# A two-layer decoder trunk: one more left pair and three more right pairs by seven products, runs of sixteen products in conv and gate, second heads three ticks later

## The chip, the cores and the metric

The kernel runs on one core of a Trainium2 chip. The metric is the device time of one execution in microseconds; lower is better. The core has five engines that run their own instruction streams side by side and wait for one another by semaphores: TensorE (PE in the profile; PEld is its weight load), VectorE (DVE), ScalarE (ACT), GpSimd (POOL) and SyncE (SP), which here only issues transfers. Matmuls write to PSUM, a small memory that this kernel divides into eight tiles of 128 x 512 fp32 values (two double tiles `mm2`, three tiles `bank`, one `av`); everything else on the chip lies in SBUF.

## The reference

Two layers; in each the same five steps on 256 tokens of width 2048:

```python
h = _rmsnorm(x, attn_norm_g[l])
proj = h @ w_in[l]
q, k, v, gate_b, gate_c, conv_in = jnp.split(proj, splits, axis=-1)
...
attn = _diff_attention(q, k, v, lam, rel_bias)
...
conv = gate_b * _short_conv(gate_c * conv_in, conv_w[l])
...
x = x + jnp.concatenate([attn, conv.astype(attn.dtype)], axis=-1) @ w_out[l]
...
hm = _rmsnorm(x, mlp_norm_g[l]) @ w_up[l]
x = x + jnp.square(jax.nn.relu(hm)) @ w_down[l]
```

q, k and v are 1024 wide each (8 heads), and so are gate_b, gate_c and conv_in. w_up is 2048 x 8192, w_down 8192 x 2048. All data is fp32 in HBM.

## The kernel before

**Precision.** TensorE multiplies in fp32r. Every operand is split into a rounded part (hi) and what is left (lo), and a product is three matmuls: hi by hi, hi by lo, lo by hi (`TERMS`). A weight tile is loaded by SP, ACT copies it to hi (L302 for most weights, L818 and L844 in the MLP), and DVE subtracts to get lo (L303, L819, L845). `Weights.take()` hands the next pair of tiles to the matmuls and makes tiles some way ahead.

**Ticks.** Work that is not a weight product (norms, transposes, attention) is written as generators. `work.start(generator, wait)` adds one, and each call of `work.tick()` between groups of matmuls steps those that are due. So a number of ticks says behind how many groups of matmuls a piece of side work is put in TensorE's order. The framework orders the instructions of ACT and DVE by itself; each engine runs its order strictly.

**The mixer** (`mixer`, `linear`, `linear_t`). First q, k and v for heads 0 to 3, then for heads 4 to 7 (`linear`, L386). `attention` is started for each half; its scores are matmuls at L604, its softmax output goes through the av matmuls (L648), `an` (L668) and transposes at L677 into `cat` (L681, L682). Then four times gate_C (`gc`) and conv_in (`ci`), and four times gate_B (`gb`), all by `linear_t` (matmuls at L408): per weight tile of four k, eight hi matmuls of 512 columns and eight lo matmuls of 256 columns, with four ticks. The output projection `o` ends the mixer. The second half's attention starts 9 ticks after it is queued (3 + 6 x half).

**The MLP** (`mlp`). The 8192 hidden units are 32 pairs (`NP`) of 2 x 128. For each pair two up columns (`up_part`, L955, runs of sixteen hi and sixteen lo matmuls) give the squared relu in `square` (L972 to L988), which writes h and splits it into f, hi by ACT at L987 and lo by DVE at L988. The left half of the output (columns 0 to 1023) is accumulated along the way, `LAG` = 2 pairs behind: pair j by seven products (Strassen-Winograd on 2 x 2 blocks, 7 x 3 = 21 matmuls, L998, the weight sums made by DVE and split into `b1`, `b2`, `t13`, `t24`), and the last two pairs, 30 and 31, by `ordinary` (L1079, 8 x 3 = 24 matmuls). Products 1 and 6 share one PSUM tile. Between them `seven_onto(0)` (L1058 to L1070) adds the seven accumulators to x: `e1` by ACT at L1060, the others by DVE (L1052), and x += e at L1068.

**The right half** (columns 1024 to 2047). Every pair's f (or h) was stored to DRAM by POOL's queue and comes back as `fb` or `back`. First pairs 30 and 31, then 2 x `BLK` pairs, then the rest of the hidden units as blocks of two pairs for one half of the right columns at a time (`columns`, L1161, 24 matmuls and 4 ticks each). `SEVEN` lists the pairs that go by seven products; the rest go by `ordinary`. Before, `BLK_AT` = (13, 14): layer 0 has 26 pairs, of which 10 by seven, and the blocks (13,0), (14,0), (13,1), (14,1); layer 1 has 28 pairs, of which 11 by seven, and (14,0), (14,1). In layer 0 the transposes of the next layer's norm (`Norm.chunk`, L454, 8 transposes a chunk into two buffers of the PSUM pool `bank`, which holds three) come among these blocks and the next q projection; `nT` (ACT L270, DVE L271) reads them out of PSUM. Chunks 0 and 1 are of the left half and are started with 4 and 8 ticks ahead of the blocks; chunks 2 and 3 are started when the blocks of their half are done, and wait 5 and 2 ticks. A chunk waits 2 ticks of its own after its start where no other number is written.

**SBUF shared between stages.** `uraw`, the raw tiles of w_up, lie in a pool that is opened for the MLP, in memory that the mixer's temporaries held. SP issues a load when its memory is free, and holds the loads behind it in program order meanwhile.

Of the kernel before, what the change touches and what calls it, by code (L numbers as in the profile page):

```python
# [30 lines left out]
KG = 4  # L31
# [3 lines left out]
LAG = 2  # L35
NB2 = DFF // (KG * P)


SEVEN_AT = (2, 4, 7, 9, 12, 14, 17, 19, 22, 24, 27)
BLK_AT = (13, 14)  # L40

TERMS = ((0, 0), (0, 1), (1, 0))
REL = 2 * S - P - 1
# [62 lines left out]
def trunk(ctx: ExitStack, tc: tile.TileContext, x, w_in, w_out, conv_w, q_norm_g, k_norm_g,  # L106
# [285 lines left out]
    def linear_t(name, acts, weights):  # L392

        acc = mm.tile([P, 2, 2, S], F32, tag="mm2", name=name)
        nk = len(acts) * KG
        for k0 in range(0, nk, 4):
            hi, lo = weights.take()  # L400
            a = acts[k0 // KG]
            while not a.ready:
                work.tick()
            for part, wt in ((0, hi), (1, lo)):
                for k in range(k0, k0 + 4):
                    for f in range(2):
                        fs = slice(f * P, (f + 1) * P)
                        nc.tensor.matmul(  # L408
                            acc[:, f, 0] if part else acc[:, f], wt[:, k % 4, fs],
                            a.ap[:, 0, k % KG] if part else a.ap[:, :, k % KG],  # L410
                            start=(part == 0 and k == 0), stop=(part == 1 and k == nk - 1),
                            skip_group_check=True)
                    if k % 2:
                        work.tick()
        return acc

# [299 lines left out]
    def mixer(l, norm, loads):  # L716

        with ExitStack() as scope:
# [28 lines left out]
            for half in range(2):  # L747
                h0 = 4 * half
                acc = linear(f"q{l}{half}", hT, weights)
                r = norm.r  # L750
                qT = bpool.tile([P, 2, 4, S], F32R, tag="b", name=f"qT{l}{half}")
                work.start(qk_norm(acc, r, q_parts(qT), q_gain[:, l:l + 1], f"q{l}{half}"))
                acc = linear(f"k{l}{half}", hT, weights)
                kT = bpool.tile([P, 2, 4, S], F32R, tag="b", name=f"kT{l}{half}")
                work.start(qk_norm(acc, r, k_parts(kT, kL), k_gain[:, l:l + 1], f"k{l}{half}"))
                acc = linear(f"v{l}{half}", hT, weights)
                v = bpool.tile([P, 2, NT, CH], F32R, tag="b", name=f"v{l}{half}")
                for t in range(NT):
                    nc.scalar.activation(v[:, 0, t], acc[:, t], AF.Copy, scale=r[:, t:t + 1])
                    nc.vector.scalar_tensor_tensor(v[:, 1, t], acc[:, t], r[:, t:t + 1],  # L760
                                                   v[:, 0, t].bitcast(F32),
                                                   op0=ALU.mult, op1=ALU.subtract)
                work.start(attention(l, qT, kT, kL, v, h0, cat[half], bias, tmp,
                                     1 + half), 3 + 6 * half)
            cv = bpool.tile([P, AW // P, S], F32, tag="b", name=f"cv{l}")
            for q in range(AW // WC):
                acc = linear_t(f"gc{l}{q}", hT, weights)
# [22 lines left out]
    def mlp(l, mnorm, last):  # L790

        norm = None if last else Norm(0, l + 1)
        BLK = BLK_AT[l]
        SEVEN = [i for i in SEVEN_AT if i < 2 * BLK]
        mT = mnorm.tiles
        with ExitStack() as scope:
            upool = scope.enter_context(tc.tile_pool(name="upool", bufs=4))
# [86 lines left out]
            for i in range(NP):  # L884
# [6 lines left out]
                for c in range(2):  # L891
                    column(i, c, 0)
                    column(i, c, 1)
                    if i >= LAG:
                        weights.jobs += (pair[2:], pair[:2])[c == 0]
            for i in range(NP - LAG, NP):
                box = []
                rows(i, 0, box)
                rows(i, 1, box)

# [65 lines left out]
            def square(i, h):  # L968


                u = h[:, 0:4].rearrange("p a c -> p (a c)")
                nc.scalar.activation(u, u, AF.Relu)  # L972
                top = h[:, 0:4].rearrange("p (k t) c -> p k t c", t=2)[:, :, 0]
                nc.vector.tensor_mul(top, top,
                                     mnorm.ratio.unsqueeze(1).to_broadcast([P, 2, P]))
                nc.scalar.activation(u, u, AF.Square)
                n = 4
                if i < NP - LAG:
                    n = 8
                    nc.vector.tensor_add(h[:, S1], h[:, A21], h[:, A22])  # L980
                    nc.vector.tensor_sub(h[:, S2], h[:, S1], h[:, A11])
                    nc.vector.tensor_sub(h[:, S3], h[:, A11], h[:, A21])
                    nc.vector.tensor_sub(h[:, S4], h[:, A12], h[:, S2])
                if i in SEVEN:
                    nc.gpsimd.dma_start(hid7[i], h.rearrange("p a c -> p (a c)"))
                f = fpool.tile([P, 2, 8, P], F32R, tag="f", name="f")
                nc.scalar.activation(f[:, 0, :n], h[:, :n], AF.Copy)  # L987
                nc.vector.tensor_sub(f[:, 1, :n], h[:, :n], f[:, 0, :n].bitcast(F32))  # L988
                if i in hid:
                    nc.gpsimd.dma_start(hid[i], f[:, :, 0:4].rearrange("p a k c -> p a (k c)"))  # L990
                return f
# [3 lines left out]
            def product(n, f, a, b, start, stop):  # L995

                for m, (pa, pw) in enumerate(TERMS):
                    nc.tensor.matmul(prods[n], f[:, pa, a], b[pw],  # L998
                                     start=(start and m == 0), stop=(stop and m == 2))

            fs = {}
            for i in range(NP):
                j = i - LAG
                end = i == NP - 1
                h = fpool.tile([P, 8, P], F32, tag="h", name="h", bufs=2)
                if i == 0:
                    two = mm.tile([P, 2, CH], F32, tag="mm2", name="up0")
# [10 lines left out]
                for c in range(2):  # L1018
# [8 lines left out]
                    if j == 0 and c == 0:  # L1027
# [2 lines left out]
                            prods[pair[0]], prods[pair[1]] = w2[:, 0], w2[:, 1]  # L1030
                        for n in (5, 7, 4):
                            prods[n] = bank(f"pr{l}{n}")
                    if j >= 0 and c == 0:
                        b11, b21, b22 = weights.take()
                        t1, t3 = weights.take()
                        f = fs[j]
                        product(1, f, A11, b11, j == 0, end)
                        product(2, f, A12, b21, j == 0, False)
                        product(3, f, S4, b22, j == 0, False)
                        product(5, f, S1, t1, j == 0, end)  # L1040
                        work.tick()
                    elif j >= 0:
                        t2, t4 = weights.take()
                        f = fs[j]
                        product(7, f, S3, t3, j == 0, end)
                        product(6, f, S2, t2, j == 0, end)
                        product(4, f, A22, t4, j == 0, False)
                        work.tick()


            def onto(dst, p, base):
# [20 lines left out]
            def ordinary(f, starts=(), stop=False):  # L1072


                for k in range(2):
# [6 lines left out]
                                stop=(stop and k == 1 and m == 2))  # L1082
                    work.tick()

            add = seven_onto(0)
            prods[8] = ps.tile([P, CH], F32, tag="av", name=f"pr{l}8", bufs=1)
            for j in range(NP - LAG, NP):
                ordinary(fs[j], (8,) if j == NP - LAG else (), j == NP - 1)
            add()
            for n in range(2):  # L1090
                for t in range(NT):
# [176 lines left out]
```

## Time and profile before

| | |
|---|---|
| runs | 2133.83, 2133.86, 2135.43 us, median 2133.86 |
| the profiled execution | 2133.02 us, span of the trace 2131.2 us |
| busy share of the span | PE 100%, PEld 85%, DVE 79%, ACT 63%, POOL 8% |
| DMA | 476.01 MB, mean 223 GB/s, q1 (SP) 60.5%, q0 (POOL) 10.1% |

The span runs from the first to the last instruction in the trace; the execution's time has 1.8 us more around it. In rows of the timeline the columns are start in us from the span's start, duration in us, engine, line, operation, output<-inputs by the program's names, shapes and count; in square brackets stands idle time of that engine ahead of it and what ended it. Matmuls are pipelined: a duration of 0.39 for a 512-column matmul is longer than the distance of two of them. Of the waits, the columns are total in us, times, and the longest.

### The profile page before, as it was taken

The numbers are of one execution on the slowest core, as the hardware profiler recorded it, in microseconds if no ns is written. First come the engines' busy times: TensorE is split into PE (matmuls) and PEld (weight loads), VectorE is DVE, ScalarE is ACT, GpSimd is POOL, SyncE is SP. The second block draws the span as 40 slices with busy tenths as digits, with TensorE's granted clock in tenths as the row PEclk, the third lists the DMA queues.
The fourth block names the chain that finished last, engine by engine and source line by source line (L and its number), as shares of the span: only waits on it lengthen the run. The fifth ranks groups of instructions, "written<-read, shape, count | busy, mean of one in ns | idle before, by whom it ended". The sixth has DMA issues, their size and how long they took to land.

```text
span 2131.2 us, 29207 instructions
## 1 busy us (share of the span) xinstructions
PE 2125.1 (100%) x10925; PEld 1818.4 (85%) x10925; DVE 1693.9 (79%) x2316; ACT 1349.2 (63%) x1776; POOL 165.6 (8%) x226
## 2 busy tenths in 40 slices
PE   9999999999999999999999999999999999999999
PEld 8888888888888888888888888888888888888887
DVE  6778655798888888798766786557988888888986
ACT  6666545677777777656565665446777777675654
POOL 3110100000000000011111101000000000000110
PEclk9999999999999999999999999999999999999999
DMA  8555766677777777788656558656877777777983
GB/s 271 178 166 167 252 193 187 206 252 229 230 236 229 233 235 229 255 297 287 216 170 182 163 162 264 188 178 211 259 231 233 232 235 229 236 229 259 319 297 112
DMA packets 298255, 476.01 MB, mean 223 GB/s; under 512 B 12708, under 2 KB 193782, under 8 KB 298113
## 3 DMA queue, kind: packets, MB, share of 16 engines
q1 hardware_dynamic: 269120, 406.76, 60.5%
q0 software_dynamic: 28800, 67.24, 10.1%
q8 instruction: 85, 1.39, 0.3%
q14 instruction: 58, 0.47, 0.1%
q10 hardware_dynamic: 192, 0.15, 0.0%
HBM read 440.52 MB, written 33.58 MB: 222 GB/s over the span
## 4 chain that ended last, share of the span: by engine, by line
PE 99%; ACT 1%; DVE 0%; issue 0%; DVEq 0%; ACTq 0%
PE upc L955 31%; PE pr L998 14%; PE dn L1079 8%; PE o L386 8%; PE ci L408 4%; PE gb L408 4%; PE k L386 4%; PE q L386 4%; PE v L386 4%; PE gc L408 4%; PE dn L1161 2%; PE dn L998 2%; PE pr1r L998 1%; PE pr0r L998 1%; PE up L955 1%; PE upw L955 1%
## 5 line engine op out<-in xcount | busy, mean ns | idle before, releaser
L303 DVE TENSOR_TENSOR wlo<-raw,whi 128x1024 fp32r<-128x1024 f32 x274 | 343.0, 1252 | 217.8 <-ACT whi L302 213.6
L302 ACT ACTIVATE whi<-raw 128x1024 fp32r<-128x1024 f32 x274 | 290.4, 1060 | 303.3 <-PE o L386 73.6
L955 PE MATMUL upc<-nT,uhi 128*128 128x512 f32 x1920 | 454.7, 389 | 0.0
L955 PEld LDWEIGHTS upc<-nT,uhi 128*128 128x128 f32 x1920 | 360.3, 188 | 74.7
L819 DVE TENSOR_TENSOR ulo<-uraw,uhi 128x1024 fp32r<-128x1024 f32 x256 | 311.9, 1222 | 119.1 <-ACT f L987 91.4
L818 ACT ACTIVATE uhi<-uraw 128x1024 fp32r<-128x1024 f32 x256 | 270.5, 1057 | 159.9 <-PE upc L955 137.5
L955 PEld LDWEIGHTS upc<-nT,ulo 128*128 128x128 f32 x1920 | 246.2, 191 | 9.3
L955 PE MATMUL upc<-nT,ulo 128*128 128x256 f32 x1920 | 249.1, 283 | 0.0
L1079 PE MATMUL dn<-whi,fb 128*128 128x512 f32 x528 | 166.1, 389 | 0.0
L386 PE MATMUL o<-whi,cat 128*128 128x512 f32 x512 | 159.5, 390 | 0.0
L302 ACT ACTIVATE whi<-uraw 128x1024 fp32r<-128x1024 f32 x66 | 70.1, 1062 | 94.0 <-PE dn L1079 77.5
L1079 PEld LDWEIGHTS dn<-whi,fb 128*128 128x128 f32 x528 | 99.1, 188 | 20.6
L844 ACT ACTIVATE b2h<-draw 128x1024 fp32r<-128x1024 f32 x81 | 85.9, 1061 | 45.9 <-PE pr L998 41.3
L386 PEld LDWEIGHTS o<-whi,cat 128*128 128x128 f32 x512 | 96.2, 188 | 19.7
L965 ACT ACTIVATE ev<-upc 128x512 f32<-128x512 f32 x120 | 72.0, 600 | 54.1 <-PE upc L955 54.1
L1079 PE MATMUL dn<-wlo,fb 128*128 128x512 f32 x264 | 102.7, 389 | 0.0
L303 DVE TENSOR_TENSOR wlo<-uraw,whi 128x1024 fp32r<-128x1024 f32 x66 | 80.7, 1223 | 24.8 <-ACT whi L302 24.5
L844 ACT ACTIVATE t24h<-t 128x1024 fp32r<-128x1024 f32 x81 | 86.2, 1064 | 22.2 <-PE pr L998 15.8
L845 DVE TENSOR_TENSOR b2l<-draw,b2h 128x1024 fp32r<-128x1024 f32 x81 | 98.5, 1217 | 1.7 <-ACT b2h L844 1.7
L845 DVE TENSOR_TENSOR t24l<-t,t24h 128x1024 fp32r<-128x1024 f32 x81 | 98.7, 1219 | 1.3
L386 PE MATMUL o<-wlo,cat 128*128 128x512 f32 x256 | 99.6, 389 | 0.0
L845 DVE TENSOR_TENSOR t13l<-t,t13h 128x1024 fp32r<-128x1024 f32 x81 | 98.7, 1219 | 1.1
(408 smaller groups left out, 4153.3 us busy)
## 6 DMA issues: line engine op xcount, KB each, us to landing
uraw<-in_w_up_dram SPq DMA_DIRECT2D x128, 1024.0 KB, 6.2
raw<-in_w_in_dram SPq DMA_DIRECT2D x191, 512.0 KB, 3.8
draw<-in_w_down_dram SPq DMA_DIRECT2D x170, 512.0 KB, 5.2
uraw<-in_w_down_dram SPq DMA_DIRECT2D x66, 512.0 KB, 5.3
raw<-in_w_out_dram SPq DMA_DIRECT2D x64, 512.0 KB, 3.6
hid0p<-f POOLq DMA_DIRECT2D x20, 512.0 KB, 3.6
raw<-in_w_down_dram SPq DMA_DIRECT2D x10, 1024.0 KB, 5.1
fb<-hid0p POOLq DMA_DIRECT2D x20, 512.0 KB, 7.4
```

What stands on the lines that cost most here:

```text
L302: pair = (nc.scalar.activation(hi, raw, AF.Copy), nc.vector.tensor_sub(lo, raw, hi.bitcast(F32)))
L303: nc.vector.tensor_sub(lo, raw, hi.bitcast(F32)))
L386: nc.tensor.matmul(acc[:, t], a.ap[:, pa, k % KG, t * P:(t + 1) * P], (hi, lo)[pw][:, j], start=(k == 0 and n == 0), stop=(k == nk - 1 and ...
L408: nc.tensor.matmul(acc[:, f, 0] if part else acc[:, f], wt[:, k % 4, fs], a.ap[:, 0, k % KG] if part else a.ap[:, :, k % KG], start=(part ...
L818: pair = (nc.scalar.activation(hi, src, AF.Copy), nc.vector.tensor_sub(lo, src, hi.bitcast(F32)))
L819: nc.vector.tensor_sub(lo, src, hi.bitcast(F32)))
L844: keep(nc.scalar.activation(hi, src, AF.Copy))
L845: keep(nc.vector.tensor_sub(lo, src, hi.bitcast(F32)))
L955: nc.tensor.matmul(acc[:, 0] if part else acc, wt[part][:, k], a.ap[:, 0, k % KG] if part else a.ap[:, :, k % KG], start=(part == 0 and kh ...
L965: nc.scalar.activation(ev, acc, AF.Copy)
L998: nc.tensor.matmul(prods[n], f[:, pa, a], b[pw], start=(start and m == 0), stop=(stop and m == 2))
L1079: nc.tensor.matmul(prods[p], f[:, pa, 2 * k + t], b[pw][:, n], start=(p in starts and k == 0 and m == 0), stop=(stop and k == 1 and m == 2))
```

## The change

Five edits. The right half's list of pairs by seven products is one for both layers, with twelve, and `BLK` is 14 in both. The left half's pair 30 goes by seven products; the products of one pair are moved into a function `some`, which is called for pair 30 behind the loop and ahead of `seven_onto(0)`, and only pair 31 goes by `ordinary`. `square` makes the sums S1 to S4 for pair 30 as well. `linear_t` takes two weight tiles, does their sixteen hi and then their sixteen lo matmuls, and ticks eight times in that stretch, six of these in the hi part. The second half's attention starts 12 ticks after it is queued. Behind the pairs layer 0 has the blocks (14,0) and (14,1) alone; the start and wait of the norm's chunks stay as written. Line numbers of the changed kernel are 2 higher from `linear_t`'s end on, and 4 higher behind `some`.

```diff
--- before.py
+++ after.py
@@ -36,8 +36,8 @@
 NB2 = DFF // (KG * P)
 
 
-SEVEN_AT = (2, 4, 7, 9, 12, 14, 17, 19, 22, 24, 27)
-BLK_AT = (13, 14)
+SEVEN = (2, 4, 6, 9, 11, 13, 16, 18, 20, 23, 25, 27)
+BLK = 14
 
 TERMS = ((0, 0), (0, 1), (1, 0))
 REL = 2 * S - P - 1
@@ -396,13 +396,15 @@
 
         acc = mm.tile([P, 2, 2, S], F32, tag="mm2", name=name)
         nk = len(acts) * KG
-        for k0 in range(0, nk, 4):
-            hi, lo = weights.take()
-            a = acts[k0 // KG]
-            while not a.ready:
-                work.tick()
-            for part, wt in ((0, hi), (1, lo)):
-                for k in range(k0, k0 + 4):
+        for k0 in range(0, nk, 8):
+
+            tiles = [weights.take() for _ in range(2)]
+            for part in range(2):
+                for k in range(k0, k0 + 8):
+                    a = acts[k // KG]
+                    while not a.ready:
+                        work.tick()
+                    wt = tiles[(k - k0) // 4][part]
                     for f in range(2):
                         fs = slice(f * P, (f + 1) * P)
                         nc.tensor.matmul(
@@ -410,7 +412,7 @@
                             a.ap[:, 0, k % KG] if part else a.ap[:, :, k % KG],
                             start=(part == 0 and k == 0), stop=(part == 1 and k == nk - 1),
                             skip_group_check=True)
-                    if k % 2:
+                    if k % 4 == 3 or (part == 0 and k % 2 == 0):
                         work.tick()
         return acc
 
@@ -761,7 +763,7 @@
                                                    v[:, 0, t].bitcast(F32),
                                                    op0=ALU.mult, op1=ALU.subtract)
                 work.start(attention(l, qT, kT, kL, v, h0, cat[half], bias, tmp,
-                                     1 + half), 3 + 6 * half)
+                                     1 + half), 3 + 9 * half)
             cv = bpool.tile([P, AW // P, S], F32, tag="b", name=f"cv{l}")
             for q in range(AW // WC):
                 acc = linear_t(f"gc{l}{q}", hT, weights)
@@ -790,8 +792,6 @@
     def mlp(l, mnorm, last):
 
         norm = None if last else Norm(0, l + 1)
-        BLK = BLK_AT[l]
-        SEVEN = [i for i in SEVEN_AT if i < 2 * BLK]
         mT = mnorm.tiles
         with ExitStack() as scope:
             upool = scope.enter_context(tc.tile_pool(name="upool", bufs=4))
@@ -893,10 +893,11 @@
                     column(i, c, 1)
                     if i >= LAG:
                         weights.jobs += (pair[2:], pair[:2])[c == 0]
-            for i in range(NP - LAG, NP):
-                box = []
-                rows(i, 0, box)
-                rows(i, 1, box)
+            for make in quarters(NP - 2):
+                weights.jobs.append(make)
+            box = []
+            rows(NP - 1, 0, box)
+            rows(NP - 1, 1, box)
 
 
 
@@ -975,7 +976,7 @@
                                      mnorm.ratio.unsqueeze(1).to_broadcast([P, 2, P]))
                 nc.scalar.activation(u, u, AF.Square)
                 n = 4
-                if i < NP - LAG:
+                if i < NP - 1:
                     n = 8
                     nc.vector.tensor_add(h[:, S1], h[:, A21], h[:, A22])
                     nc.vector.tensor_sub(h[:, S2], h[:, S1], h[:, A11])
@@ -998,10 +999,27 @@
                     nc.tensor.matmul(prods[n], f[:, pa, a], b[pw],
                                      start=(start and m == 0), stop=(stop and m == 2))
 
+            def some(j, c, t3):
+
+                f, first, end = fs[j], j == 0, j == NP - 2
+                if c:
+                    t2, t4 = weights.take()
+                    product(7, f, S3, t3, first, end)
+                    product(6, f, S2, t2, first, end)
+                    product(4, f, A22, t4, first, False)
+                else:
+                    b11, b21, b22 = weights.take()
+                    t1, t3 = weights.take()
+                    product(1, f, A11, b11, first, end)
+                    product(2, f, A12, b21, first, False)
+                    product(3, f, S4, b22, first, False)
+                    product(5, f, S1, t1, first, end)
+                work.tick()
+                return t3
+
             fs = {}
             for i in range(NP):
                 j = i - LAG
-                end = i == NP - 1
                 h = fpool.tile([P, 8, P], F32, tag="h", name="h", bufs=2)
                 if i == 0:
                     two = mm.tile([P, 2, CH], F32, tag="mm2", name="up0")
@@ -1030,22 +1048,8 @@
                             prods[pair[0]], prods[pair[1]] = w2[:, 0], w2[:, 1]
                         for n in (5, 7, 4):
                             prods[n] = bank(f"pr{l}{n}")
-                    if j >= 0 and c == 0:
-                        b11, b21, b22 = weights.take()
-                        t1, t3 = weights.take()
-                        f = fs[j]
-                        product(1, f, A11, b11, j == 0, end)
-                        product(2, f, A12, b21, j == 0, False)
-                        product(3, f, S4, b22, j == 0, False)
-                        product(5, f, S1, t1, j == 0, end)
-                        work.tick()
-                    elif j >= 0:
-                        t2, t4 = weights.take()
-                        f = fs[j]
-                        product(7, f, S3, t3, j == 0, end)
-                        product(6, f, S2, t2, j == 0, end)
-                        product(4, f, A22, t4, j == 0, False)
-                        work.tick()
+                    if j >= 0:
+                        forms["t3"] = some(j, c, forms.get("t3"))
 
 
             def onto(dst, p, base):
@@ -1082,10 +1086,10 @@
                                 stop=(stop and k == 1 and m == 2))
                     work.tick()
 
+            some(NP - 2, 1, some(NP - 2, 0, None))
             add = seven_onto(0)
             prods[8] = ps.tile([P, CH], F32, tag="av", name=f"pr{l}8", bufs=1)
-            for j in range(NP - LAG, NP):
-                ordinary(fs[j], (8,) if j == NP - LAG else (), j == NP - 1)
+            ordinary(fs[NP - 1], (8,), True)
             add()
             for n in range(2):
                 for t in range(NT):
```

## The prediction

> **What bounds the kernel now.** I read, in this order: busy time by engine with the clock, the chain of waits by engine, and the waits of TensorE.
>
> ```profile
> PE 2125.1 (100%) x10925; PEld 1818.4 (85%) x10925; DVE 1693.9 (79%) x2316; ACT 1349.2 (63%) x1776; POOL 165.6 (8%) x226
> ...
> PEclk9999999999999999999999999999999999999999
> ...
> PE 99%; ACT 1%; DVE 0%; issue 0%; DVEq 0%; ACTq 0%
> ```
> ```profile
> PE sc L604 <- DVE cat L682: 1.2, 2, 0.6
> PE warm L160 <- DVE mhalf L152: 1.1, 1, 1.1
> ```
>
> TensorE is busy all the time, at full clock, and the chain lies on it. After the start it waits twice, 0.6 us each, ahead of the scores L604 of a second attention half. So matmuls taken away shorten the run one for one, and a new wait of TensorE lengthens it one for one. There is no slack to pay with.
>
> **Fewer matmuls.** The price comes from a chain piece of nothing but 512-column matmuls.
>
> ```profile
> 912.43 10.88 PE dn L1079 x48
> ```
>
> 10.88/48 = 0.2267 us each. An ordinary pair is 24 matmuls (4 accumulators x 2 k x 3 terms); a pair by seven products 21. More pairs go by seven: left, pair 30 in each layer (2); right, 12 pairs in each layer instead of 10 and 11 (3). 5 x 3 = 15 matmuls, 3.40 us. The operand work for these goes to ACT and DVE; where the new right pairs stand (two apart at the closest), a period is 21 + 24 matmuls, 10.2 us, and DVE has in it seven operations on 128x1024 (t, three lo parts of the weights, the lo part of f, and two wlo of the ordinary pair) and three on 128x512. Back to back these are 1.14 and 0.6 apart:
>
> ```profile
> 887.74 2.36 DVE L303 TENSOR_TENSOR wlo<-draw,whi 128x1024 fp32r<-128x1024 f32 x2 [4.97 <-issue]
> ...
> 895.53 1.29 DVE L1068 TENSOR_TENSOR x<-x,e 128x512 f32<-128x512 f32 x2
> ```
>
> 7 x 1.14 + 3 x 0.6 = 9.8 us, so DVE stays 0.4 us a period inside TensorE's time, at no cost; one more 0.6 operation would uncover 0.2 us a period.
>
> **Runs of sixteen.** gc, ci and gb take two weight tiles at once, 16 hi and then 16 lo matmuls.
>
> ```profile
> 255.86 2.00 PE L408 MATMUL gb<-nT,whi 128*128 128x512 f32 x8
> ...
> 267.03 1.32 PE L408 MATMUL gb<-nT,whi 128*128 128x512 f32 x5
> ```
> ```profile
> 422.16 5.54 PE upc L955 x32
> ```
>
> Four tiles of 8 + 8 take (267.03 - 255.86)/4 = 2.79 each. A run of 16 + 16 in the up columns takes 5.54: 16 x 0.2267 leaves 0.120 per lo matmul. 8 x 0.2267 + 8 x 0.120 = 2.77, so a change from lo back to hi costs about 0.02. There are 24 calls of four tiles and two changes go in each: 48 x 0.02 = 0.96 us.
>
> **Second heads.** They start 3 ticks later in the projection, so that the waits of scores on `cat` should go: 2 x 0.61 = 1.21 us (the first row of the waits). The gains sum to 3.40 + 0.96 + 1.21 = 5.57.
>
> **Left end: a wait of `e1` and f.** Pair 30 now goes by seven products; what comes behind is one ordinary pair instead of two. These are the engines around the end of the left half in layer 0.
>
> ```profile
> 890.03 0.69 ACT L1060 ACTIVATE e<-pr,rowf 128x512 f32<-128x512 f32 x1 [0.79 <-PE pr L998]
> ...
> 892.47 0.63 ACT L976 ACTIVATE h<-h 128x512 f32<-128x512 f32 x1 [1.24 <-DVE h L974]
> 893.14 0.63 ACT L987 ACTIVATE f<-h 128x512 fp32r<-128x512 f32 x1
> ```
> ```profile
> 890.75 0.75 DVE L1052 SCALAR_TENSOR_TENSOR e<-pr,rowf,e 128x512 f32<-128x512 f32 x1 [0.32 <-ACT e L1060]
> 891.42 0.68 DVE L1068 TENSOR_TENSOR x<-x,e 128x512 f32<-128x512 f32 x1
> ...
> 894.93 0.69 DVE L988 TENSOR_TENSOR f<-h,f 128x512 fp32r<-128x512 f32 x1
> ```
> ```profile
> 889.60 0.61 PE L998 MATMUL pr<-t24h,f 128*128 128x512 f32 x2
> ...
> 890.51 0.39 PE L1079 MATMUL pr<-whi,f 128*128 128x512 f32 x1
> ```
>
> `e1` reads product 1, which lies in one tile with product 6, so it waits for the last matmul of product 6 (889.60 + 0.39, `e1` at 890.03). With pair 30 by seven products that matmul is the 18th behind 890.51: 890.51 + 17 x 0.2267 = 894.36, so `e1` starts at 894.79. In the changed program's order on ACT the copy to f of pair 31 (f hi) stands behind `e1`; on DVE f lo stands behind `e2` and one x += e1. So: `e1` to 895.48, f hi to 896.01 (0.69, 0.63, starts overlapping by 0.1); `e2` from 895.52, x from 896.19, f lo from 896.78 to 897.47. The ordinary pair 31 is due at 890.51 + 21 x 0.2267 = 895.27, and its third matmul, the first to read f lo, at 895.72. It gets it 1.75 us late. Before, pair 31 came 24 matmuls behind pair 30, f lo was due at 896.40 and done at 895.62. If f lo came ahead of the x addition it would be 0.68 less, 1.1; with one more of DVE's 0.75 operations ahead 2.5. The layers have one order: 2 x 1.8 = 3.6, bounds 2.2 and 5.0. What is queued behind `e1` on ACT (the weight copies for the right half) is due 24 matmuls later, and is covered.
>
> **Layer boundary: eight ticks where there were sixteen.** With BLK 14 in layer 0 only the blocks (14,0) and (14,1) lie behind the pairs. The transposes of the four chunks of the next norm were spread over four blocks and the q projection.
>
> ```profile
> 1055.08 1.03 PE L454 MATMUL tpn<-ident,x 128*128 128x128 f32 x8
> ...
> 1061.41 1.03 PE L454 MATMUL tpn<-ident,x 128*128 128x128 f32 x8
> ...
> 1066.38 1.03 PE L454 MATMUL tpn<-ident,x 128*128 128x128 f32 x8
> ...
> 1071.35 0.39 PE L386 MATMUL q<-whi,nT 128*128 128x512 f32 x1
> ...
> 1074.08 1.03 PE L454 MATMUL tpn<-ident,x 128*128 128x128 f32 x8
> ```
> ```profile
> 1055.27 1.06 ACT L302 ACTIVATE whi<-raw 128x1024 fp32r<-128x1024 f32 x1 [1.66 <-PE dn L1161]
> 1056.24 0.82 ACT L270 ACTIVATE nT<-tpn,ngains 128x256 fp32r<-128x256 f32 x2
> ```
> ```profile
> 1057.51 0.87 DVE L271 SCALAR_TENSOR_TENSOR nT<-tpn,ngains,nT 128x256 fp32r<-128x256 f32 x2
> ...
> 1058.93 1.40 DVE L1052 SCALAR_TENSOR_TENSOR x<-dn,rowf,x 128x512 f32<-128x512 f32 x2
> ...
> 1060.64 1.22 DVE L303 TENSOR_TENSOR wlo<-raw,whi 128x1024 fp32r<-128x1024 f32 x1
> ```
>
> They were 5 to 7.7 us apart; each fills two PSUM buffers of the three named `bank`, which nT on ACT and then DVE empties. By the ticks written in the code chunk 0 comes at tick 6, chunk 2 at 9, chunks 1 and 3 both at 10: six buffers wanted within two ticks of 6 matmuls (2.7 us). Put T = 0 at the first matmul of (14,0). Two blocks of 24 matmuls and chunk 0's transposes (0.9) end at 11.8. Behind (14,1) ACT does a whi (1.06) that waited for the buffer this block frees, then nT (0.82); DVE does x twice (1.40), that whi's wlo (1.22) and only then chunk 0's nT (0.87), to 15.1. TensorE does one tick of q and the first half of chunk 2 to 13.5, and needs the bank then: 1.6 us of idle. Likewise the first half of chunk 3 waits 0.3 for chunk 2's nT, and the second half 2.7 for chunk 1's, behind another whi and wlo. Sum 4.6, once. If each long wait were one wlo (1.22) shorter, 2.1; one whi (1.06) longer, 6.7.
>
> **The prefetch of w_up.** Its four 1 MB loads go into memory that the attention's temporaries hold, so SP issues them behind the last `an` of the second heads, and the projection's own weights queue behind them.
>
> ```profile
> 231.54 1.29 DVE L668 TENSOR_TENSOR an<-ao,af 128x512 f32<-128x512 f32 x2
> ```
> ```profile
> 247.30 1.06 ACT L302 ACTIVATE whi<-raw 128x1024 fp32r<-128x1024 f32 x1 [1.72 <-DMA raw<-in_w_in_dram]
> 251.46 1.06 ACT L302 ACTIVATE whi<-raw 128x1024 fp32r<-128x1024 f32 x1 [3.09 <-DMA raw<-in_w_in_dram]
> ```
> ```profile
> 250.27 2.00 PE L408 MATMUL ci<-nT,whi 128*128 128x512 f32 x8
> ...
> 253.06 2.00 PE L408 MATMUL ci<-nT,whi 128*128 128x512 f32 x8
> ```
> ```profile
> 1310.43 1.06 ACT L302 ACTIVATE whi<-raw 128x1024 fp32r<-128x1024 f32 x1 [2.92 <-DMA raw<-in_w_in_dram]
> ```
> ```profile
> 1312.29 2.00 PE L408 MATMUL ci<-nT,whi 128*128 128x512 f32 x8
> ```
>
> Layer 0: the last ci tile's whi is ready at 252.52 for 253.06, 0.54 us to spare. The change takes this twice. Hi of both tiles comes first, so it is due 8 matmuls behind 250.27, 1.81, which is 252.08 (251.9 with the saved change), 1.1 earlier. And the attention is 3 ticks later; through POOL's and DVE's order I follow `an` to be 1.4 later, and with it the four loads and all that queues behind them. 252.52 + 1.4 - 251.9 = 2.0 us. In layer 1 the margin is 1312.29 - 1311.49 = 0.80, 0.26 more: 1.75. Sum 3.75. If the landings don't move, 0.6 and 0.35, some 1.0; moved by the whole three ticks (1.85, with the av matmuls), 2.5 + 2.2 = 4.7.
>
> **The sum.** 3.6 + 4.6 + 3.75 = 11.95 lost against 5.57 won: +6.4. The profiled execution took 2133.02 (span 2131.2 and 1.8 around it), so 2139.4 there. The median of the runs is 0.84 above it: 2140.2, which I forecast as 2140.
>
> **The rivals.**
>
> The count alone: every new wait is hidden. For it: the left end's order and the boundary's are read from the program, and a few hundred nanoseconds on ACT decide each; against it: three places would have to be wrong, and the prefetch margin is 0.54 us in a row of the trace. 2133.86 - 5.57 = 2128.3, faster. It decides if f of pair 31 is ready by 895.3, the banks by their ticks and the whi by 251.9.
>
> The waits come at their lower bounds: 2.2 + 2.1 + 1.0 = 5.3 against 5.57, 2133.6, no change. For it: queues on ACT and DVE may drain faster than I follow them; landings may not move with `an`, since the weights behind the loads are bounded by the queue, not by its first issue.
>
> The waits come at their upper bounds: 5.0 + 6.7 + 4.7 = 16.4, 2133.86 + 10.8 = 2144.7. For it: a late chunk makes later whi late too.
>
> An idle that costs clock: if the boundary's two long waits made the clock fall to half for as long as they last together (1.6 + 2.7 = 4.3 us), 2.2 us more are lost: 2142.4. No row bears it out: the clock row has full speed throughout, and the longest wait behind the start is 0.6. [...]
>
> The added products may bring a bound of their own: DVE behind TensorE where right pairs by seven stand two apart, 0.2 us a period with one operation of 0.6 more than I counted; with the seven such neighbours of a layer twice that is 3 us, so 2143. Against it: before shows such neighbours with no wait.
>
> **How the numbers follow.** Forecast, each wait about as sized (2136 to 2144.5): 0.62. Lower bounds: 0.19. Count alone: 0.07. Upper bounds and DVE: 0.09. Clock: 0.03. Range: from below the lower-bound case, 2132, to the upper-bound case, 2145. The likeliest's own range is 2136 to 2144.5. A measurement of this kernel can tell about 0.2% from no change, 4.3 us: faster is below 2129.6, which the count alone reaches: 0.07. Within: the lower bounds and the foot of the forecast up to 2138.1, 0.19 + 0.07 = 0.26. Slower: 0.67.
>
> **What would show it.** 15 matmuls less, and no wait of sc on cat. New waits of TensorE: on ACT's and DVE's f at the ordinary pair 31 in both layers (1.8 each); on DVE's nT at the transposes at the boundary, layer 0 only (two long ones, 1.6 and 2.7); on whi at the last ci tile, about 252 and 1311 (2.0, 1.75). gb in runs of 5.57 instead of 5.59. The forecast is wrong if the sum of TensorE's new waits is under 8 us, or if the w_up landings do not move.

## The result and the profile after

The changed kernel takes 2144.44 us (median of six runs, 2141.82 to 2145.48) against 2133.68 of before in the same comparison: a ratio of 1.005 with an interval of 1.004 to 1.006. It is slower. The profiled execution took 2144.81 us with a span of 2143.0, 11.8 above the span of before.

The busy times by engine and the chain by engine, as shown of before:

```profile
PE 2125.6 (99%) x10910; PEld 1817.4 (85%) x10910; DVE 1710.2 (80%) x2352; ACT 1362.5 (64%) x1789; POOL 159.7 (7%) x226
...
PE 98%; DMA 1%; DVE 0%; ACT 0%; issue 0%; DVEq 0%; ACTq 0%
```

There are 15 matmuls fewer, and TensorE is still as long busy as before (2125.6 against 2125.1). So there are two things to find: idle time that was not there, and matmuls that became slower. The waits of TensorE (total in us, times, longest):

```profile
PE ci L410 <- ACT whi L302: 5.9, 4, 2.0
PE tpn L456 <- DVE nT L271: 3.9, 2, 2.5
PE pr L1083 <- DVE f L989: 1.5, 2, 0.7
PE pr L1083 <- ACT f L988: 1.2, 2, 0.6
PE warm L160 <- DVE mhalf L152: 1.1, 1, 1.1
```

The scores' wait on `cat` is gone. In its place stand three groups, in just the places that the prediction named. Where the 11.9 us lie is best read from the starts of the first matmul of each stage, taken from both traces (lengths in us):

| stage | before | after | difference |
|---|---|---|---|
| start to the first gc | 156.06 | 156.30 | +0.24 |
| gc and ci, layer 0 | 99.80 | 104.40 | +4.60 |
| gb, layer 0 | 44.69 | 44.53 | -0.16 |
| o, layer 0 | 89.75 | 89.76 | +0.01 |
| up and left half, layer 0 | 511.09 | 512.46 | +1.37 |
| right half to gc of layer 1 | 313.91 | 317.23 | +3.32 |
| gc and ci, layer 1 | 99.79 | 101.80 | +2.01 |
| gb and o, layer 1 | 134.44 | 134.29 | -0.15 |
| up and left half, layer 1 | 511.09 | 512.45 | +1.36 |
| right half of layer 1 to the last matmul | 166.76 | 166.08 | -0.68 |

The last row has no wait in it and shows the change at work: one more right pair by seven products, 3 x 0.2267 = 0.68 us. The gb row shows the runs of sixteen: 0.16 for four calls.

**The left end** in layer 0, on ACT, DVE and TensorE of the changed kernel:

```profile
899.60 0.69 ACT L1064 ACTIVATE e<-pr,rowf 128x512 f32<-128x512 f32 x1
900.18 0.62 ACT L988 ACTIVATE f<-h 128x512 fp32r<-128x512 f32 x1
```
```profile
900.32 0.75 DVE L1056 SCALAR_TENSOR_TENSOR e<-pr,rowf,e 128x512 f32<-128x512 f32 x1 [1.45 <-ACT e L1064]
900.99 0.68 DVE L1072 TENSOR_TENSOR x<-x,e 128x512 f32<-128x512 f32 x1
901.59 0.68 DVE L989 TENSOR_TENSOR f<-h,f 128x512 fp32r<-128x512 f32 x1
```
```profile
900.86 0.50 PE L1083 MATMUL pr<-whi,f 128*128 128x512 f32 x1 [0.62 <-ACT f L988]
901.19 0.40 PE L1083 MATMUL pr<-wlo,f 128*128 128x512 f32 x1
902.33 0.73 PE L1083 MATMUL pr<-whi,f 128*128 128x512 f32 x2 [0.74 <-DVE f L989]
```

f hi starts behind `e1`, f lo behind `e2` and one x += e, and the pair 31 waits for the one and then for the other. The second wait costs more than its bracket says. From 901.19 to 902.33 are 1.14 us where two matmuls lie 0.23 apart, so 0.91 for a bracket of 0.74 (with 0.39 of length and 0.23 of distance a matmul's end stands 0.16 behind the next one's start), and the matmul behind it is again some 0.1 late. This wait costs its bracket and about 0.27.

**The layer boundary**, on TensorE and DVE:

```profile
1077.63 0.63 PE L456 MATMUL tpn<-ident,x 128*128 128x128 f32 x4 [1.40 <-DVE nT L271]
...
1079.49 1.76 PE L456 MATMUL tpn<-ident,x 128*128 128x128 f32 x12
1083.77 0.63 PE L456 MATMUL tpn<-ident,x 128*128 128x128 f32 x4 [2.52 <-DVE nT L271]
```
```profile
1075.87 1.22 DVE L303 TENSOR_TENSOR wlo<-raw,whi 128x1024 fp32r<-128x1024 f32 x1
1077.01 1.26 DVE L271 SCALAR_TENSOR_TENSOR nT<-tpn,ngains,nT 128x256 fp32r<-128x256 f32 x3
```

The transposes stand in two heaps within 9 us, and each heap ends in a wait for DVE's nT, which stands behind a wlo.

**The last ci tiles** of layer 0, on ACT and TensorE:

```profile
250.06 1.06 ACT L302 ACTIVATE whi<-raw 128x1024 fp32r<-128x1024 f32 x1 [3.85 <-DMA raw<-in_w_in_dram]
254.20 1.06 ACT L302 ACTIVATE whi<-raw 128x1024 fp32r<-128x1024 f32 x1 [3.08 <-DMA raw<-in_w_in_dram]
```
```profile
251.17 2.11 PE L410 MATMUL ci<-nT,whi 128*128 128x512 f32 x8 [1.46 <-ACT whi L302]
255.31 2.92 PE L410 MATMUL ci<-nT,whi 128*128 128x512 f32 x8 [2.02 <-ACT whi L302]
```

ACT sits idle for the transfer both times. The landings are 2.75 us later than before (247.30 to 250.06, 251.46 to 254.20). And eight matmuls that took 2.11 take 2.92. The stretch behind, in the view by windows (busy us of PE, PEld, DVE, ACT and POOL with counts, then the granted clock, DMA share and GB/s):

```profile
250.00:256.00 6.00, 2.80 (x11) 2.03 (x12) 1.94 (x2) 2.58 (x3) 0.00 (x0) 1.00 1.00 340
256.00:260.00 4.00, 4.00 (x18) 3.54 (x17) 1.74 (x2) 2.71 (x3) 0.00 (x0) 0.57 0.64 184
```

TensorE's clock is 0.57 for 4 us: 4 x 0.43 = 1.7 us lost. These are the matmuls that became slower.

### The profile page after: what moved, and what is told of

Its sections match the earlier page's. It is cut to its first block, busy times and chain, and to the rows that moved or that the text cites. A ratio compares the mean times of both kernels' runs of the same rounds, so it can differ in the third digit from the quotient of the medians.

```text
span 2143.0 us, 29238 instructions
## 1 busy us (share of the span) xinstructions
PE 2125.6 (99%) x10910; PEld 1817.4 (85%) x10910; DVE 1710.2 (80%) x2352; ACT 1362.5 (64%) x1789; POOL 159.7 (7%) x226
## 4 chain that ended last, share of the span: by engine, by line
PE 98%; DMA 1%; DVE 0%; ACT 0%; issue 0%; DVEq 0%; ACTq 0%
PE upc L956 31%; PE pr L999 14%; PE o L386 8%; PE dn L1083 8%; PE gc L410 4%; PE gb L410 4%; PE k L386 4%; PE v L386 4%; PE q L386 4%; PE ci L410 4%; PE dn L999 2%; PE dn L1165 2%; PE pr1r L999 2%; PE pr0r L999 2%; PE up L956 1%; PE upw L956 1%
## 5 line engine op out<-in xcount | busy, mean ns | idle before, releaser
L303 DVE TENSOR_TENSOR wlo<-raw,whi 128x1024 fp32r<-128x1024 f32 x270 | 327.4, 1223 | 222.3 <-ACT whi L302 158.0
L302 ACT ACTIVATE whi<-raw 128x1024 fp32r<-128x1024 f32 x270 | 286.0, 1060 | 295.1 <-PE o L386 73.6
L1083 PE MATMUL dn<-whi,fb 128*128 128x512 f32 x512 | 161.5, 389 | 0.0
L844 ACT ACTIVATE b2h<-draw 128x1024 fp32r<-128x1024 f32 x86 | 91.3, 1062 | 50.0 <-PE pr L999 42.0
L844 ACT ACTIVATE t24h<-t 128x1024 fp32r<-128x1024 f32 x86 | 91.4, 1063 | 23.5 <-PE pr L999 16.5
L845 DVE TENSOR_TENSOR t24l<-t,t24h 128x1024 fp32r<-128x1024 f32 x86 | 104.8, 1219 | 1.8
L845 DVE TENSOR_TENSOR b2l<-draw,b2h 128x1024 fp32r<-128x1024 f32 x86 | 104.6, 1217 | 1.3 <-ACT b2h L844 1.3
L845 DVE TENSOR_TENSOR t13l<-t,t13h 128x1024 fp32r<-128x1024 f32 x86 | 104.8, 1219 | 0.8
L858 DVE TENSOR_TENSOR t<-draw 128x1024 f32<-128x1024 f32 x86 | 104.8, 1219 | 0.4
L844 ACT ACTIVATE t13h<-t 128x1024 fp32r<-128x1024 f32 x86 | 91.5, 1064 | 13.5 <-DVE t L858 2.9
```

The source lines that it names most:

```text
L302: pair = (nc.scalar.activation(hi, raw, AF.Copy), nc.vector.tensor_sub(lo, raw, hi.bitcast(F32)))
L303: nc.vector.tensor_sub(lo, raw, hi.bitcast(F32)))
L844: keep(nc.scalar.activation(hi, src, AF.Copy))
L845: keep(nc.vector.tensor_sub(lo, src, hi.bitcast(F32)))
L858: keep(nc.vector.tensor_sub(t[:, 0:2], raw[:, :, 1], raw[:, 0]))
L1083: nc.tensor.matmul(prods[p], f[:, pa, 2 * k + t], b[pw][:, n], start=(p in starts and k == 0 and m == 0), stop=(stop and k == 1 and m == 2))
```

## The experiments

The two mixer edits are taken apart first, then the transfer, the left end and the boundary, and then what is left is put together. Each comparison ran beside the kernel before (2133.3 to 2133.5 in these).

### The changed kernel once more

> The changed kernel once more, for its spread and for a second profile. [...] 2142 to 2145.5.

2143.27 us (ratio 1.0046, 1.0033 to 1.0059). Nearly the same waits at ci in layer 0, 1.40 and 1.96; behind them, by windows:

```profile
250.00:256.00 6.00, 2.92 (x12) 2.11 (x13) 2.06 (x2) 2.64 (x3) 0.00 (x0) 1.00 0.99 343
256.00:260.00 4.00, 4.00 (x27) 3.62 (x26) 3.28 (x4) 3.26 (x4) 0.00 (x0) 1.00 0.63 184
```

The same four microseconds hold 27 matmuls, not 18, at full clock, and the stage is 102.74 long, not 104.40. So the waits of this place cost 1.7 us more in the one execution than in the other.

### Second heads at 9 ticks

```diff
-                                     1 + half), 3 + 9 * half)
+                                     1 + half), 3 + 6 * half)
```

> The changed kernel with the second heads started 9 ticks late as before; runs of sixteen kept. Theory A (the later heads delay `an`, so the four w_up loads and the projection's weights behind them land late): landings go back to where they were, the two waits at the last ci tiles shrink from 1.46 + 2.03 and 0.43 + 1.97 us to at most 0.6 and 0.35 (sixteen hi matmuls want their second tile 1.1 us earlier than before), TensorE's clock does not fall, and the scores' two waits of 0.6 come back: 2144.4 - 8.8 + 1.3 + 1.3 = 2138. Theory B (only the runs of sixteen, which want hi sooner, make the waits): the ci waits stay and 1.2 is added, 2145.6.

2150.07 us (ratio 1.0079, 1.0067 to 1.0092), beyond both expectations. Its waits:

```profile
PE ci L410 <- ACT whi L302: 7.8, 2, 4.1
...
PE sc L606 <- DVE cat L684: 1.0, 2, 0.5
```

Undoing this edit makes the ci waits larger: one of 4.14 in layer 0, one of 3.70 in layer 1, and the clock falls at each: 0.50 over 250 to 256 and 0.62 over 1320 to 1326 (the eight matmuls of 512 columns behind each wait take 3.78 us, the eight ahead of it 2.00); by windows in layer 0:

```profile
250.00:256.00 6.00, 5.24 (x16) 4.47 (x17) 2.45 (x2) 3.88 (x4) 0.00 (x0) 0.50 0.66 211
```

SP's own queue shows why, first in the changed kernel, then in this one (start, time in issue, transfer, count):

```profile
227.34 5.51 SPq L343 DMA_DIRECT2D raw<-in_w_in_dram  x2
233.75 3.95 SPq L811 DMA_DIRECT2D uraw<-in_w_up_dram  x3
237.80 3.98 SPq L343 DMA_DIRECT2D raw<-in_w_in_dram  x1
241.82 1.63 SPq L811 DMA_DIRECT2D uraw<-in_w_up_dram  x1
```
```profile
227.57 1.47 SPq L343 DMA_DIRECT2D raw<-in_w_in_dram  x2
232.42 6.61 SPq L811 DMA_DIRECT2D uraw<-in_w_up_dram  x4
239.12 8.07 SPq L343 DMA_DIRECT2D raw<-in_w_in_dram  x4
```

With runs of sixteen and 9 ticks all four loads of w_up stand ahead of the next weight tile; at 12 ticks a tile of w_in is let in between. With runs of sixteen the later heads do not make these waits, they ease them. My theory A had the wrong edit.

### Conv and gate in runs of eight

```diff
-        for k0 in range(0, nk, 8):
-            tiles = [weights.take() for _ in range(2)]
...
+        for k0 in range(0, nk, 4):
+            hi, lo = weights.take()
```

> The changed kernel with conv and gate in runs of eight as before; second heads stay at 12 ticks. Theory A (late landings): the first ci wait stays in each layer (1.5 and 0.4), the second shrinks by 1.1 to about 0.9 in each, the clock does not fall (1.7), and the 48 changes from lo to hi come back (0.94): 2144.4 - 2.2 - 1.7 + 0.9 = 2141.4. Theory B (runs of sixteen alone): the ci waits are gone, 2144.4 - 8.8 + 0.9 = 2136.5.

2138.10 us (1.0022, 1.0012 to 1.0032), between the two. One wait of 0.98 is left at ci in layer 0 and 0.03 in layer 1. The 0.98 is near what the prediction would give for the later heads alone (1.4 less the margin of 0.54 that before had, 0.86), but it does not come by the prediction's way: `an` (L668) starts at 231.22 here, 0.32 earlier than before, and the last ci tile's whi still starts 1.17 later (252.63 for 251.46). The rest of the ci waits came with the runs of sixteen.

### Both mixer edits undone

> The changed kernel with both mixer edits undone (runs of eight, second heads at 9 ticks): the fourth corner of the two. Theory A' (with runs of sixteen only two tiles stand ahead of the w_up loads on SP where there were three, and the later heads only shift the block of loads): the ci waits are gone, sc waits 0.6 twice are back: against runs of eight at 12 ticks (2138.1) one wait of 0.98 with its restart (0.27) goes and 2 x 0.87 comes: 2138.6. Theory A (the later heads make the waits): the same place, but then 9 ticks with runs of sixteen should have been better than 12, and it was not. A time below 2137 would say that the later heads cost more than their waits show.

2140.24 us (1.0031, 1.0020 to 1.0041). No wait at ci; the scores' two waits of 0.59 are back. That is 1.6 above the expectation, which had no fall of the clock in it; the profiled execution has a mean granted clock of 0.999, where runs of eight at 12 ticks have 1.000. This fourth corner leaves the two edits in this form: at runs of eight the later heads are no loss (2138.1 against 2140.2). In the two profiles they are no gain either: gc and ci of both layers take 199.69 at 12 ticks and 199.54 at 9, and the 1.8 us between the spans lie at the layer boundary (317.09 at 12 ticks and 318.85 at 9), which with the mean clocks of 1.000 and 0.999 points to a fall of the clock there. At 9 ticks the runs of sixteen cost 10 us, at 12 ticks 5 to 6.

### The first loads of w_up behind w_out's

```diff
+            behind = [loads[-32 + n] for n in (4, 10, 16, 22)]
...
+                        if i < 2:
+                            with tc.issue_after(behind[2 * i + kh].ins):
+                                nc.sync.dma_start(raws[kh], src)
```

> The changed kernel with one thing moved: SP issues the four first 1 MB loads of w_up behind the 5th, 11th, 17th and 23rd load of w_out, not among the loads of conv and gate. Theory A (the ci waits are a queue of transfers): no ci wait in either layer, no fall of the clock: 2144.4 - 5.9 idle - 1.7 clock - 0.16 for each of four restarts = 2136.1; a wait at up if 1 MB is now late there, some 0 to 3 us. Theory B (the waits are of ACT or of the attention's order): waits unchanged, 2144.4.

`tc.issue_after(x)` puts what its block issues behind x in the queue of x's engine, and adds no other wait; `loads` holds the loads of the mixer's weights in order.

2137.36 us (1.0017, 1.0008 to 1.0026). With both mixer edits in place, and nothing moved but four loads in SP's queue, no ci wait is left in either layer, and none comes at the up columns. Waits left:

```profile
PE tpn L458 <- DVE nT L271: 3.9, 2, 2.5
PE pr L1090 <- DVE f L996: 1.5, 2, 0.7
PE pr L1090 <- ACT f L995: 1.2, 2, 0.6
```

gc and ci take 98.83 us in both layers, against 104.40 and 101.80: the place cost 5.57 and 2.97. It was a queue of transfers. The time is 1.3 above the expectation, which had no fall of the clock in it; the profile has one, at the boundary this time (0.63 over the 4 us around the end of the second wait, 4 x 0.37 = 1.5):

```profile
1076.00:1080.00 4.00, 2.60 (x9) 2.24 (x10) 2.52 (x7) 2.18 (x5) 0.00 (x0) 0.63 0.41 133
```

The next four stand on this kernel.

### Left pair 30 by ordinary products

The edit takes back `some(NP - 2, ...)`, `quarters(NP - 2)` and the longer sums in `square`, so that pairs 30 and 31 are both ordinary.

> On the kernel with w_up's first loads behind w_out's (2137.4): pair 30 of the left half by ordinary products as before, six matmuls more. Theory A (the left edit costs more than it saves): the two waits a layer on f of pair 31 (0.62 and 0.74, with the restart behind each and the delay some 2.05 in all) go, 3 x 0.2267 = 0.68 comes back in each layer: 2137.4 - 2 x 1.37 = 2134.6. Theory B (these waits are hidden elsewhere, the right half's start would wait instead): 2137.4 + 1.4 = 2138.8.

2134.43 us (1.0003, 0.9995 to 1.0012), 2.9 less, as theory A had it. Up and left half are 511.09 long again in both layers.

### f of pair 31 ahead of e1

```diff
-            add = seven_onto(0)
+            with tc.issue_after(split[0].ins), tc.issue_after(split[1].ins):
+                add = seven_onto(0)
```

(`split` holds the two instructions that make f.)

> On the kernel with w_up's first loads behind w_out's (2137.4): only the order on ACT and DVE is changed, f of pair 31 stands ahead of e1 and e2. Theory A (it is a question of order, not of work): ACT's f hi is ready at about the time it is due, f lo some 0.4 late, so a wait of 0.3 to 0.8 a layer is left of 2.05: 2137.4 - 2 x 1.4 = 2134.6. Theory B (the squares of pair 31 are late themselves, as its up columns end only 21 matmuls ahead): the waits stay above 1 a layer, 2136.5 or more; or the accumulators that e1 and e2 free come late, and dn waits instead.

2135.57 us (1.0010, 1.0001 to 1.0019), 1.8 less: most of it, but not all. The waits on f shrink to 0.01. The stage is 511.11 long, though, no shorter than with ordinary products and 0.7 above what 21 matmuls should make it: f comes just at the time it is due, and a delay of under 0.16 a matmul (0.39 of length less 0.23 of distance) shows no idle. Four of the first matmuls of pair 31 start 0.11 to 0.17 late each, 0.56 in all. And a new wait stands in the right half:

```profile
PE dn L1175 <- DVE wlo L305: 0.6, 2, 0.3
```

The sums onto x are now later on DVE, and a wlo of the right half behind them with them.

### The norm's chunks spaced

```diff
-                work.start(norm.chunk(0, 2), 4)
-                work.start(norm.chunk(1, 2), 8)
+                work.start(norm.chunk(0, 2), 1)
+                work.start(norm.chunk(1, 2), 4)
...
-                        work.start(norm.chunk(2 + n, (5, 2)[n]))
+                        work.start(norm.chunk(2 + n, (6, 6)[n]))
```

> On the kernel with w_up's first loads behind w_out's (2137.4): the four norm chunks at the layer boundary at ticks 3, 6, 10 and 14 instead of 6, 9, 10 and 10. Theory A (three PSUM buffers asked for six times in two ticks): the waits of the transposes on nT (1.40, 0.09, 2.53, with restarts 4.7) go, and with them the fall of the clock that can follow them (1.7): 2131.0 to 2132.7. Theory B (ACT and DVE are behind there whatever the spacing, since the seven products' sums hold the buffers until 3 to 4 us into the blocks): new waits of 1 to 3 us at chunk 0 or later, 2134 to 2136.

2131.20 us (0.9990, 0.9981 to 0.9998), 6.2 less. No wait is left at the transposes, and no buffer comes late at tick 3. The stretch from the right half to gc of layer 1 is 312.52, against 317.23 in the changed kernel: the place cost 4.71, and the profile of the kernel that this one stands on had a fall of the clock on top (the 0.63 over 4 us above). With it the spread goes: eleven runs lie between 2130.83 and 2131.70, where the kernel without it had 2135.96 to 2138.28.

### All three mended, and all but the left edit

> w_up's first loads behind w_out's, f ahead of e1, and the chunks spaced. If the three causes are independent and the count of matmuls is paid as priced (3.40 + 0.96 + 1.21 and the restarts 0.3, less the waits left at the left end, some 1.2): 2133.4 - 4.7 = 2128.7, faster than before by 0.2%. If the causes hide one another, the savings overlap and it stays above 2131.

2129.90 us (0.9983, 0.9974 to 0.9992). 1.2 short of the expectation, and that is the left edit.

> w_up's first loads behind w_out's, chunks spaced, and pair 30 of the left half by ordinary products as before. If the left edit does not pay even with f ahead (its stage then took 511.1 us, as with ordinary products, and a wait of dn on wlo of 0.28 came), this beats all three mended (2129.9) by about 0.5 to 0.9 us a layer: 2128.2 to 2129.0. If the left edit pays once mended, this is 1.4 slower: 2131.3.

2128.37 us (0.9974, 0.9964 to 0.9985), the fastest. TensorE's waits in the whole run:

```profile
PE warm L160 <- DVE mhalf L152: 1.1, 1, 1.1
```

Even with f ahead the left edit loses 0.8 us a layer against ordinary products. Up and left half take the same time both ways (511.11 and 511.09); it is the right half that is longer, 313.09 against 312.51 in layer 0 and 166.72 against 166.08 in layer 1, where dn waits for the wlo.

> As the one before, with the second heads at 9 ticks instead of 12. With the w_up loads out of the way the only thing the 3 ticks can do is to spare the scores' wait on cat: 0.6 with a restart of 0.27, twice, so 1.7 slower than at 12 ticks. If the later heads are worth nothing by themselves, the two are equal within 0.3.

2129.54 us (0.9980, 0.9971 to 0.9988). The scores wait 0.52 twice again. The three ticks are worth 1.2 us, as long as the loads are out of the way. That is less than the 1.7 expected: a wait of 0.52 makes gc and ci only 0.58 longer (99.41 against 98.83), not 0.52 + 0.27.

## Why the prediction was right

Right were the direction, the range and all three places; the size fell short: 6.4 us were forecast on the profiled execution, and 11.8 came. That the median of 2144.44 still lies within the likeliest range (to 2144.5) and the whole one (to 2145) is in part luck: of the six runs three are above the one and two above the other, and a fall of the clock that came in this profile, and not in the next one of the same kernel, is worth 1.7.

- **Fewer matmuls, 3.40**: as priced, 0.68 for each right pair in the row of the last stage. DVE stayed inside TensorE's time: the best kernel has all twelve right pairs and no wait there.
- **Runs of sixteen, 0.96**: as priced, 0.16 for four calls and so 0.96 for 24.
- **Second heads, 1.21**: 1.17 by the last two runs.
- **Left end, 3.6 in both layers**: the order on ACT and DVE and the wait for product 6 were as described. 512.46 - 511.09 + 0.68 = 2.05 a layer were lost, 4.1 in all. The waits were shorter than 1.8 (1.36 in brackets), but the sum took a wait as its idle time alone, and each cost about 0.3 more ((2.05 - 1.36)/2).
- **Layer boundary, 4.6**: 4.7, with the brackets 1.40, 0.09 and 2.52 where 1.6, 0.3 and 2.7 were forecast. The idle time is 4.0; that the sums meet is luck, since the forecast had no price for starting again behind a wait.
- **Prefetch of w_up, 3.75**: 8.54 (5.57 and 2.97). This is the term that was mis-sized, above its own upper bound of 4.7. Three things were wrong in it. It moved `an`, and with it the landings, by 1.4. `an` moved by 0.83 (from 231.54 to the row below), and so did the first load of w_up on SP (232.92 to 233.75), but the landings by 2.75 by the clock of the trace, while TensorE came 1.3 earlier (gc03 ended at 243.42, not 244.68): 4 on TensorE's axis. So the tile before the last came late too, with waits of 1.46 and 0.43 that the prediction didn't have. It blamed the later heads for the shift; the runs showed that the runs of sixteen make most of it and that, beside them, the later heads ease it (gc and ci of both layers take 206.20 at 12 ticks and 212.51 at 9). And a fall of the clock took 1.7 (0.57 over 4 us).

```profile
232.37 1.29 DVE L670 TENSOR_TENSOR an<-ao,af 128x512 f32<-128x512 f32 x2
```

17.34 lost less 5.57 won are 11.8, the difference of the spans. In idle time alone the brackets of the new waits make 12.61 (2.72 at the left end, 4.01 at the boundary, 5.88 at ci) where 11.95 were forecast; two terms were too large and one too small, so this near meeting is luck as well. The rest is what the sum had no term for: some 0.27 behind each of eleven waits, 3.0, and the clock, 1.7.

Of the rivals, the upper bounds (2144.7) came nearest in time, but not by their way: the left end and the boundary stood near the middle, and one place alone ran over. The clock was a rival with 0.03 and at the boundary's waits; it fell behind the ci waits in the profiled execution. At the boundary it was 1.00 there (1076 to 1090), and fell in the profile with w_up's loads moved (0.63 over 4 us), behind waits of which the longest was 2.5. No run shows a clock at half for just as long as the waits last together, from which that rival's 2.2 us came; what the profiled execution shows is 3.41 us at 0.50, which is 1.7. DVE as a bound and the count alone are refuted by the best kernel and by the result.

What stays open: why the second 1 MB load of w_up took longer in the changed kernels than in before, which is a part of the 2.75 (between 240 and 246 us the DMA engines moved 325 GB/s where they had moved 357, at a busy share of 1.02 and 1.06); and why a run of sixteen puts fewer tiles ahead of these loads was read from SP's queue, and not tried with another number of raw buffers.

## What to carry to other kernels

On an engine that is busy all the time a saving of 0.7 us is easily lost to a new order on a neighbour (at the left end 0.68 a layer against 2.05): look up, for each instruction that the change makes TensorE wait on, what stands ahead of it in its engine's queue, and move that, before the work itself is undone. With the prefetch and the norm's chunks this paid; at the left end it did not, and undoing the edit was better. Large prefetches in the queue that also feeds the current stage have a price that a few ticks more or less elsewhere can raise to several microseconds (gc and ci of both layers took 197.66 us with these loads behind w_out's, and 206.20 and 212.51 at 12 and 9 ticks without); put them behind loads that are not urgent. An edit must be priced with the others in place: the later heads were worth 1.2 us with the loads moved, and the runs of sixteen cost ten us or five to six depending on them.

## What the runs showed of the hardware

**At some of TensorE's waits the granted clock fell.** In the changed kernel's profile it was 0.50 for 3.41 us, from 256.35 on, behind the ci waits of 1.46 and 2.02 in layer 0:

```profile
256.35:259.76 3.41, 3.41 (x14) 3.04 (x13) 1.39 (x2) 2.36 (x3) 0.00 (x0) 0.50 0.64 193
```

This cost 1.7 us (3.41 x 0.5). Behind the ci waits of 0.43 and 1.97 in layer 1 the clock was 1.00 (1310 to 1370), and so it was behind 1.40 and 1.96 in layer 0 in the profile of the changed kernel once more (256 to 260). At the single waits of 4.14 and 3.70, with 9 ticks and runs of sixteen, it fell both times: 0.50 over 250 to 256, and 0.62 and 0.72 over 1320 to 1326 and 1326 to 1330. At the boundary's two waits (3.9 us in all, the longest 2.5) the view of 1060 to 1120 shows a clock of 0.97 in three of seven profiles (9 ticks with runs of sixteen, w_up's first loads moved, left pair 30 by ordinary products), and of 1.00 in the other four (the changed kernel in both profiles, runs of eight, f ahead of e1). Nearly the same waits had a fall in one profile and none in another; what decides it was not shown.

The runs of each kernel that has such waits spread over 1.6 to 4.6 us; those of the four without them over 0.4 to 0.9. The spread alone proves nothing, as the kernel before, with two waits of 0.6 only, spread over 2.8 in 33 runs and 4.6 in 20.

**A wait can cost more than its idle time.** At three places here it is about 0.27 us more for each: the end of a matmul of 0.39 stands 0.16 behind the start of the next, 0.23 later, and the first matmuls after the wait are some 0.1 late. The changed kernel once more loses 3.91 at its two ci waits of 1.40 and 1.96 in layer 0, the boundary 4.71 at its 4.01, the left end 2.05 at its 1.36, which is 0.2 to 0.35 for each wait. It is not so at each place: at the scores, where matmuls of 128 and 256 columns stand around the wait, a wait of 0.52 cost 0.58.
